# Batched matmul with bias and residual: a regrouped head, and x in two buffers of eight tiles

## The chip, the cores and the metric

The kernel runs on one core of a Trainium2 chip. The metric is the device time of one execution in microseconds; "time before" is the median of seven executions. TensorE (PE) does the products and the transposes, VectorE (DVE), ScalarE (ACT) and GpSimd (POOL) the elementwise work, and SyncE (SP) issues nearly all the DMA transfers.

## The reference

```python
batch, m, k, n = 16, 512, 1024, 768
# x [batch, m, k], weight [k, n], bias [n], residual [batch, m, n], all float32
np.matmul(x, weight) + bias + residual
```

## The kernel before, in words

The batch and row dimensions are flattened to M = 8192 rows. A tile is 128 rows, so there are 64 tiles; eight of them form a group S (eight groups). Row p*8 + j of a group goes to partition p, so one partition holds eight neighbouring rows of x (8 x 4 KB, contiguous in memory), and likewise of the residual (8 x 3 KB) and the output.

Per tile t the work is:

- `cast(t)`, line 90: ScalarE copies 128 x 1024 of x from float32 to bfloat16 into `xb` (a ring of four).
- `transp(t)`, lines 98 and 100: TensorE makes eight 128 x 128 transposes into `pt` in PSUM (a ring of two), and VectorE copies them to `xt` (a ring of four).
- `mms(t, i)` for the eight steps i, line 104: each step is a pair of products, 512 and 256 columns wide, that accumulate in `po` (a ring of three).
- `finish(t)`, lines 129 and 131, on VectorE. For t < 12 it writes product plus bias to `tmp`, and `pool_add(t)`, line 121, on GpSimd adds that to the residual in `ro`. For later tiles GpSimd has already added the bias to the residual, and VectorE adds the product to it.
- The finished group in `ro` is stored from there (line 82).

The weights are loaded in float32 into the buffer `w_st`, which borrows the fourth `ro` buffer, and cast to bfloat16 (`w_sb`) by `cast_w`, lines 181 and 183, on ScalarE or VectorE. The unit of W is a block c of 256 rows with two halves e.

Before, x sits in four buffers of half a group (`X_BUFS = 4`, `H = 4`, 16 KB a partition each) and each buffer is loaded by one 2 MiB transfer (line 68), except for the first ones, which are cut finer. The residual sits in four buffers of a group (line 76, 3 MiB each).

The order of work on each engine is the order of the program, written out by hand (`keep_in_program_order`). SP issues its transfers in that order too, each of them when what it needs is free: a load of x waits for the casts that read the buffer before, a load of the residual for the store of the group that used the buffer, and each also for the transfer that was issued eight transfers earlier.

The head treats tiles 0 to 2 together, since W arrives slowly: warm-up matmuls (`keep_warm`, line 175), the product that spreads the bias over the partitions (line 188, copied by VectorE at line 192), the first casts and transposes, and then step after step of W for three tiles. The head's order of transfers is: x of tile 0, W block 0 half 0, tiles 1 and 2, W block 0 half 1, W blocks 1 to 3, tiles 3, 4, 5, tiles 6 and 7 together, and then residual and x in turns up to tile 15 and residual group 1: 17 MiB in all. From tile 3 on the main loop runs: in the turn of tile t it casts t + 2, does the products of t with the transposes of t + 1 in the middle, and finishes t - 1.

Of the kernel before, what the change touches and what calls it, by code (L numbers as in the profile page):

```python
# [8 lines left out]
FP32 = mybir.dt.float32  # L9
BF16 = mybir.dt.bfloat16  # L10
P = 128
J = 8
H = 4
HEAD = 3
X_BUFS = 4
RO_BUFS = 4
TMP_BUFS = 4
EARLY = 12
# [4 lines left out]
def kernel(  # L23
# [8 lines left out]
    nc = tc.nc  # L32
# [3 lines left out]
    M, K = x2d.shape  # L36
    N = weight.shape[1]
    n_c = K // (2 * P)
    n_t = M // P
    n_s = n_t // J  # L40
# [3 lines left out]
    x_d = x2d.rearrange("(S p j) k -> S p j k", p=P, j=J)  # L44
    res_d = res2d.rearrange("(S p j) n -> S p j n", p=P, j=J)
    out_d = out2d.rearrange("(S p j) n -> S p j n", p=P, j=J)
    w_d = weight.rearrange("(c p e) n -> p c e n", p=P, e=2)

    const = ctx.enter_context(tc.tile_pool(name="const", bufs=1))
    sb = ctx.enter_context(tc.tile_pool(name="sb", bufs=1))  # L50
    ps = ctx.enter_context(tc.tile_pool(name="ps", bufs=1, space=bass.MemoryType.PSUM))

    def ring(pool, name, i, n, shape, dt):
        return pool.tile(shape, dt, name=name, tag=f"{name}{i % n}", bufs=1)

    def psum_o(i):
        return ring(ps, "po", i, HEAD, [P, N], FP32)

    x_sb, ro, xb, xt, po, tmp = {}, {}, {}, {}, {}, {}
    K_ = tc.keep_in_program_order  # L60


    def load_x(h, j0=0, j1=H):
        if h < n_t // H:
            if j0 == 0:
                x_sb[h] = ring(sb, "x_tile", h, X_BUFS, [P, H, K], FP32)
            S, b = divmod(h * H, J)
            K_(nc.sync.dma_start(
                out=x_sb[h][:, j0:j1, :], in_=x_d[S, :, b + j0:b + j1, :]
            ))  # L70

    def load_res(S, j0=0, j1=J):
        if S < n_s:
            if j0 == 0:
                ro[S] = ring(sb, "ro", S, RO_BUFS, [P, J, N], FP32)
            K_(nc.sync.dma_start(out=ro[S][:, j0:j1, :], in_=res_d[S, :, j0:j1, :]))

    def load_w(c, e0=0, e1=2):
        K_(nc.sync.dma_start(out=w_st[:, c, e0:e1, :], in_=w_d[:, c, e0:e1, :]))

    def store(S, j0=0, j1=J, n0=0, nl=N):
        K_(nc.sync.dma_start(
            out=out_d[S, :, j0:j1, n0:n0 + nl], in_=ro[S][:, j0:j1, n0:n0 + nl]
        ))


    def cast(t):
        if t < n_t:
            xb[t] = ring(sb, "xb", t, 4, [P, n_c, P, 2], BF16)
            K_(nc.scalar.copy(  # L90
                out=xb[t].rearrange("p c i e -> p (c i e)"), in_=x_sb[t // H][:, t % H, :]
            ))

    def transp(t):
        if t < n_t:
            pt = ring(ps, "pt", t, 2, [P, len(steps), P], BF16)
            for i, (c, e) in enumerate(steps):
                K_(nc.tensor.transpose(out=pt[:, i, :], in_=xb[t][:, c, :, e], identity=ident))  # L98
            xt[t] = ring(sb, "xt", t, 4, [P, len(steps), P], BF16)
            K_(nc.vector.tensor_copy(out=xt[t], in_=pt))  # L100

    def mm(t, i, n0, nl):
        c, e = steps[i]
        K_(nc.tensor.matmul(  # L104
            po[t][:, n0:n0 + nl], lhsT=xt[t][:, i, :], rhs=w_sb[:, c, e, n0:n0 + nl],
            start=(i == 0), stop=(i == len(steps) - 1),
        ))

    def mms(t, i):
        if i == 0:  # L110
            po[t] = psum_o(t)
        for n0, nl in chunks:
            mm(t, i, n0, nl)
# [4 lines left out]
    def pool_add(t):  # L118
        if 0 <= t < n_t:
            r = row(t)  # L120
            K_(nc.gpsimd.tensor_add(out=r, in0=r, in1=tmp[t] if t < EARLY else bias_sb))  # L121

    def finish(t, n0=0, nl=N):
        if t < 0:
            return
        p = po[t][:, n0:n0 + nl]
        if t < EARLY:
            tmp[t] = ring(sb, "tmp", t, TMP_BUFS, [P, N], FP32)
            K_(nc.vector.tensor_add(out=tmp[t], in0=p, in1=bias_sb))  # L129
        else:  # L130
            K_(nc.vector.tensor_add(out=row(t, n0, nl), in0=p, in1=row(t, n0, nl)))  # L131
# [4 lines left out]
    w_st = ring(sb, "ro", RO_BUFS - 1, RO_BUFS, [P, n_c, 2, N], FP32)  # L136
    w_sb = const.tile([P, n_c, 2, N], BF16, name="w_sb")

    load_x(0, 0, 1)
    load_w(0, 0, 1)  # L140
    load_x(0, 1, 2)
    load_x(0, 2, 3)
    load_w(0, 1, 2)
    load_w(1)
    load_w(2)
    load_w(3, 0, 1)
    load_w(3, 1, 2)
    load_x(0, 3, 4)
    load_x(1, 0, 1)
    load_x(1, 1, 2)  # L150
    load_x(1, 2, 4)
    load_res(0, 0, H)
    load_x(2)
    load_res(0, H, J)
    load_x(3, 0, 2)
    load_res(1, 0, H)
    load_x(3, 2, 4)
    load_res(1, H, J)

    warm = const.tile([P, 512], BF16, name="warm")  # L160
    K_(nc.vector.memset(warm, 0.0))  # L161
# [5 lines left out]
    ident = const.tile([P, P], BF16, name="ident")  # L167
    make_identity(nc, ident)
    bias_sb = const.tile([P, N], FP32, name="bias_sb")
    bias_ps = psum_o(1)  # L170
    warm_ps = psum_o(2)

    def keep_warm(n):
        for _ in range(n):
            K_(nc.tensor.matmul(  # L175
                warm_ps[:, 0:512], lhsT=warm[:, 0:P], rhs=warm, start=True, stop=True
            ))

    def cast_w(c, e, engine):
        if engine == "act":  # L180
            K_(nc.scalar.copy(out=w_sb[:, c, e, :], in_=w_st[:, c, e, :]))  # L181
        else:
            K_(nc.vector.tensor_copy(out=w_sb[:, c, e, :], in_=w_st[:, c, e, :]))  # L183


    keep_warm(6)
    for n0, nl in chunks:
        K_(nc.tensor.matmul(  # L188
            bias_ps[:, n0:n0 + nl], lhsT=ones_row, rhs=bias_row[:, n0:n0 + nl],
            start=True, stop=True,  # L190
        ))
    K_(nc.vector.tensor_copy(out=bias_sb, in_=bias_ps))  # L192
    keep_warm(4)
    cast(0)
    cast_w(0, 0, "dve")
    transp(0)
    keep_warm(3)
    cast(1)
    mms(0, 0)
    keep_warm(3)  # L200
    transp(1)
    cast(2)
    keep_warm(3)
    mms(1, 0)
    cast_w(0, 1, "dve")
    transp(2)
    mms(0, 1)
    mms(1, 1)
    mms(2, 0)
    mms(2, 1)  # L210
    cast_w(1, 1, "act")
    cast_w(1, 0, "dve")
    cast_w(2, 1, "act")
    cast_w(2, 0, "dve")
    cast_w(3, 0, "dve")
    cast_w(3, 1, "dve")
    cast(HEAD)
    load_x(X_BUFS)
    load_res(2)
    cast(HEAD + 1)  # L220
    for i in range(2, len(steps)):
        for t in range(HEAD):
# [8 lines left out]
    for t in range(HEAD, n_t):  # L231
        cast(t + 2)
        S, j = divmod(t, J)
        if (t + 2) % H == H - 1:
            load_x((t + 2) // H + X_BUFS)
            if j < H:
                load_res(S + 2)
            elif 1 <= S < n_s - 1:
                store(S - 1)
        if t < n_t - 1:  # L240
            for i in range(len(steps)):
                mms(t, i)
                if i == T_STEP:
                    transp(t + 1)
        finish(t - 1)
        if t - 1 < EARLY:
            pool_add(t - 1)
        if t + 1 >= EARLY:
            pool_add(t + 1)
        if S == n_s - 1 and j == 0:  # L250
            store(S - 1)
        if S == n_s - 1 and j == H:
            store(S, 0, H)
    t, S = n_t - 1, n_s - 1
    store(S, H, J - 1)
    po[t] = psum_o(t)
    for n0, nl in chunks:
        for i in range(len(steps)):
# [33 lines left out]
```

## Time and profile before

| | us |
|---|---|
| median of 7 executions | 214.69 |
| lowest, highest | 213.26, 219.32 |
| the profiled execution | 213.25 |
| its span in the profile | 211.5 |
| TensorE busy in the span | 201.7 (95%) |
| VectorE, ScalarE, GpSimd busy | 104.2, 69.1, 114.5 |
| bytes moved by DMA, mean rate | 87.27 MB, 413 GB/s |

The span is what the profiler sees from the first to the last event; the execution's own time is 1.75 us longer. A row of the timeline has start and busy time in us, engine, line, operation, what it writes and reads, how often, and in brackets how long the engine had stood idle and what released it. A line of the DMA queues has packets, MB, and the share of the time of 16 transfer engines.

### The profile page before, as it was taken

To read this page: it belongs to the slowest core of one execution; us is meant where nothing else is said; L and a number is where in the kernel's file an instruction comes from. 1 tells how busy PE (TensorE), PEld (TensorE's weight loads), DVE (VectorE), ACT (ScalarE), POOL (GpSimd) and SP (SyncE) were. 2 spreads that over 40 slices of the span, in tenths; PEclk is the share of its full clock that TensorE was granted. 3 is DMA by queue.
4 is the path that set the end of the run, shared out by engine and by line. 5 is a ranking of instruction groups with operands and counts; after the bars stand their busy time and mean duration, and the time that the engine had idled before them with its cause. 6 is when DMAs were issued, how large, how long until landed. Compare 5 with 4: busy or idle time off the path is not lost.

```text
span 211.5 us, 3621 instructions
## 1 busy us (share of the span) xinstructions
PE 201.7 (95%) x1529; PEld 131.3 (62%) x1559; DVE 104.2 (49%) x139; ACT 69.1 (33%) x68; POOL 114.5 (54%) x70
## 2 busy tenths in 40 slices
PE   7998999999999999999999999999999999999980
PEld 2455666666666666666666666666666666666650
DVE  0554544554455455545544554455445545544550
ACT  4435315331607233323332333233233233330000
POOL 1000097959989959910997029930599107990000
PEclk9999999999999999999999999999999999999997
DMA  6999999999999999999999999999999999999984
GB/s 216 412 414 425 436 422 422 418 435 443 418 418 445 418 429 434 412 442 417 425 420 437 435 425 429 409 451 421 408 421 428 446 415 429 406 437 425 424 341 196
DMA packets 7075, 87.27 MB, mean 413 GB/s; under 512 B 786, under 2 KB 914, under 8 KB 2579
## 3 DMA queue, kind: packets, MB, share of 16 engines
q1 hardware_dynamic: 7056, 87.03, 97.7%
q8 instruction: 12, 0.20, 0.4%
q14 instruction: 5, 0.03, 0.0%
q10 hardware_dynamic: 2, 0.00, 0.0%
HBM read 61.87 MB, written 25.17 MB: 412 GB/s over the span
## 4 chain that ended last, share of the span: by engine, by line
PE 94%; DVE 3%; issue 1%; DVEq 0%
PE po L104 78%; PE pt L98 13%; PE po L175 2%; DVE xt L100 1%; PE po L188 1%; DVE ro L131 1%; DVE bias_sb L192 0%; DVE tmp L129 0%; DVE w_sb L183 0%; DVE warm L161 0%; DVEq L131 0%
## 5 line engine op out<-in xcount | busy, mean ns | idle before, releaser
L104 PE MATMUL po<-w_sb,xt 128*128 128x256 bf16 (+1 forms) x994 | 175.1, 324 | 3.5 <-DVE ro L131 0.8
L104 PEld LDWEIGHTS <-xt 128*128 128x128 bf16 x1024 | 97.3, 98 | 61.5 <-DVE xt L100 2.0
L121 POOL TENSOR_TENSOR ro<-ro,bias_sb 128x768 f32<-128x768 f32 x52 | 92.5, 1815 | 46.3 <-DMA ro<-in_residual_dram 22.4
L90 ACT CAST xb<-x_tile 128x1024 bf16<-128x1024 f32 x64 | 65.9, 1045 | 117.2 <-PE pt L98 98.5
L100 DVE COPY xt<-pt 128x1024 bf16<-128x1024 bf16 x64 | 44.3, 692 | 94.1 <-PE pt L98 94.1
L131 DVE TENSOR_TENSOR ro<-po,ro 128x768 f32<-128x768 f32 (+2 forms) x53 | 49.4, 933 | 1.8 <-PE po L104 1.8
L98 PEld LDWEIGHTS <-xb 128*128 128x128 bf16 x512 | 34.0, 98 | 8.5
L98 PE MATMUL pt<-ident,xb 128*128 128x128 bf16 x512 | 39.0, 219 | 0.0
L121 POOL TENSOR_TENSOR ro<-ro,tmp 128x768 f32<-128x768 f32 x12 | 21.5, 1816 | 28.6 <-DMA ro<-in_residual_dram 26.2
L129 DVE TENSOR_TENSOR tmp<-po,bias_sb 128x768 f32<-128x768 f32 x12 | 11.3, 948 | 0.0
L175 PE MATMUL po<-warm 128*128 128x512 bf16 x19 | 6.2, 459 | 1.2 <-DVE warm L161 1.2
L183 DVE CAST w_sb<-ro 128x768 bf16<-128x768 f32 x6 | 3.3, 555 | 1.4 <-DMA ro<-in_weight_dram 1.4
L175 PEld LDWEIGHTS <-warm 128*128 128x128 bf16 x19 | 1.8, 110 | 3.3 <-issue 1.4
L192 DVE COPY bias_sb<-po 128x768 f32<-128x768 f32 x1 | 1.0, 957 | 4.5 <-PE po L188 4.5
L181 ACT CAST w_sb<-ro 128x768 bf16<-128x768 f32 x2 | 1.7, 832 | 2.9 <-DMA ro<-in_weight_dram 2.9
L188 PE MATMUL po<-tmp,ones_row 1*128 1x512 f32 (+1 forms) x4 | 1.8, 581 | 0.0
L188 PEld LDWEIGHTS po<-tmp,ones_row 1*128 1x128 f32 x4 | 0.9, 246 | 1.4 <-issue 1.4
L166 ACT ACT_TABLE_LOAD x1 | 1.3, 1283 | 1.3 <-PEq L276 1.3
L161 DVE MEMSET warm<- 128x256 uint32 x1 | 0.3, 272 | 0.9 <-PEq L276 0.9
masks.py:197 POOL MEMSET ident<- 128x128 bf16 x1 | 0.2, 205 | 0.3 <-POOLq L276 0.3
masks.py:199 POOL TENSOR_SCALAR_AFFINE_SELECT ident<-ident 128x128 bf16<-128x128 bf16 x1 | 0.3, 293 | 0.1
L276 POOL MEMSET const-float32-0.0<- 128x1 f32 x1 | 0.1, 98 | 0.2 <-issue 0.2
(6 smaller groups left out, 0.7 us busy)
## 6 DMA issues: line engine op xcount, KB each, us to landing
x_tile<-in_x_dram SPq DMA_DIRECT2D x13, 2048.0 KB, 23.2
out_dram<-ro SPq DMA_DIRECT2D x7, 3072.0 KB, 24.2
ro<-in_residual_dram SPq DMA_DIRECT2D x6, 3072.0 KB, 12.5
ro<-in_residual_dram SPq DMA_DIRECT2D x4, 1536.0 KB, 24.8
x_tile<-in_x_dram SPq DMA_DIRECT2D x6, 512.0 KB, 8.3
x_tile<-in_x_dram SPq DMA_DIRECT2D x3, 1024.0 KB, 22.0
ro<-in_weight_dram SPq DMA_DIRECT2D x4, 384.0 KB, 6.6
ro<-in_weight_dram SPq DMA_DIRECT2D x2, 768.0 KB, 8.5
```

What stands on the lines that cost most here:

```text
L90: K_(nc.scalar.copy(out=xb[t].rearrange("p c i e -> p (c i e)"), in_=x_sb[t // H][:, t % H, :]))
L98: K_(nc.tensor.transpose(out=pt[:, i, :], in_=xb[t][:, c, :, e], identity=ident))
L100: K_(nc.vector.tensor_copy(out=xt[t], in_=pt))
L104: K_(nc.tensor.matmul(po[t][:, n0:n0 + nl], lhsT=xt[t][:, i, :], rhs=w_sb[:, c, e, n0:n0 + nl], start=(i == 0), stop=(i == len(steps) - 1),))
L121: K_(nc.gpsimd.tensor_add(out=r, in0=r, in1=tmp[t] if t < EARLY else bias_sb))
L129: K_(nc.vector.tensor_add(out=tmp[t], in0=p, in1=bias_sb))
L131: K_(nc.vector.tensor_add(out=row(t, n0, nl), in0=p, in1=row(t, n0, nl)))
L166: K_(nc.scalar.copy(out=warm_a, in_=warm_a))
L175: K_(nc.tensor.matmul(warm_ps[:, 0:512], lhsT=warm[:, 0:P], rhs=warm, start=True, stop=True))
L181: K_(nc.scalar.copy(out=w_sb[:, c, e, :], in_=w_st[:, c, e, :]))
L183: K_(nc.vector.tensor_copy(out=w_sb[:, c, e, :], in_=w_st[:, c, e, :]))
L188: K_(nc.tensor.matmul(bias_ps[:, n0:n0 + nl], lhsT=ones_row, rhs=bias_row[:, n0:n0 + nl], start=True, stop=True,))
```

## The change

The head is regrouped:

- x of tiles 0 and 1 comes in one 1 MiB transfer with 8 KB in each partition. Tile 0 is cast by VectorE and tile 1 by ScalarE.
- Each block of W comes in one transfer with 6 KB in each partition. From each block VectorE and ScalarE cast one half; before, VectorE cast both halves of the first and the last block.
- 16 warm-up matmuls stand in front, in place of 19 spread over the head, and the bias product comes behind the transposes of tiles 0 and 1.
- Tile 2 is cast and transposed after the first two steps of tiles 0 and 1.

x then sits in two buffers of a whole group (32 KB a partition, the same memory in sum), each loaded by one 4 MiB transfer from group 2 on. The loads of x group S + 2 and residual group S + 2 are both issued in the turn of tile 8S + 5; before, the two halves of x were issued in the turns of tiles 8S + 1 and 8S + 5, the residual with the first of them, and the first such loads already in the head.

```diff
-H = 4
-X_BUFS = 4
+X_BUFS = 2
...
+    def load_x(S, j0=0, j1=J):
+        if S < n_s:
             if j0 == 0:
+                x_sb[S] = ring(sb, "x_tile", S, X_BUFS, [P, J, K], FP32)
+            K_(nc.sync.dma_start(out=x_sb[S][:, j0:j1, :], in_=x_d[S, :, j0:j1, :]))
...
+    def cast(t, engine="act"):
         if t < n_t:
             xb[t] = ring(sb, "xb", t, 4, [P, n_c, P, 2], BF16)
+            copy = nc.scalar.copy if engine == "act" else nc.vector.tensor_copy
...
-    load_x(0, 0, 1)
-    load_w(0, 0, 1)
-    load_x(0, 1, 2)
+    load_x(0, 0, 2)
+    load_w(0)
     load_x(0, 2, 3)
-    load_w(0, 1, 2)
     load_w(1)
     load_w(2)
-    load_w(3, 0, 1)
-    load_w(3, 1, 2)
+    load_w(3)
     load_x(0, 3, 4)
-    load_x(1, 0, 1)
-    load_x(1, 1, 2)
-    load_x(1, 2, 4)
-    load_res(0, 0, H)
-    load_x(2)
-    load_res(0, H, J)
-    load_x(3, 0, 2)
-    load_res(1, 0, H)
-    load_x(3, 2, 4)
-    load_res(1, H, J)
+    load_x(0, 4, 6)
+    load_x(0, 6, 8)
+    load_res(0, 0, 4)
+    load_x(1, 0, 4)
+    load_res(0, 4, 8)
+    load_x(1, 4, 6)
+    load_res(1, 0, 4)
+    load_x(1, 6, 8)
+    load_res(1, 4, 8)
...
-    bias_ps = psum_o(1)
-    warm_ps = psum_o(2)
+    warm_ps = psum_o(1)
+    bias_ps = psum_o(2)
...
-    keep_warm(6)
+    keep_warm(16)
+    cast(0, "dve")
+    cast(1)
+    transp(0)
+    transp(1)
+    cast_w(0, 0, "act")
+    cast_w(0, 1, "dve")
     for n0, nl in chunks:
         K_(nc.tensor.matmul(
             bias_ps[:, n0:n0 + nl], lhsT=ones_row, rhs=bias_row[:, n0:n0 + nl],
             start=True, stop=True,
         ))
     K_(nc.vector.tensor_copy(out=bias_sb, in_=bias_ps))
-    keep_warm(4)
-    cast(0)
-    cast_w(0, 0, "dve")
-    transp(0)
-    keep_warm(3)
-    cast(1)
     mms(0, 0)
-    keep_warm(3)
-    transp(1)
+    mms(0, 1)
+    mms(1, 0)
+    mms(1, 1)
     cast(2)
-    keep_warm(3)
-    mms(1, 0)
-    cast_w(0, 1, "dve")
     transp(2)
-    mms(0, 1)
-    mms(1, 1)
+    for c in range(1, n_c):
+        cast_w(c, 0, "dve")
+        cast_w(c, 1, "act")
     mms(2, 0)
     mms(2, 1)
-    cast_w(1, 1, "act")
-    cast_w(1, 0, "dve")
-    cast_w(2, 1, "act")
-    cast_w(2, 0, "dve")
-    cast_w(3, 0, "dve")
-    cast_w(3, 1, "dve")
     cast(HEAD)
-    load_x(X_BUFS)
-    load_res(2)
     cast(HEAD + 1)
...
-        if (t + 2) % H == H - 1:
-            load_x((t + 2) // H + X_BUFS)
-            if j < H:
-                load_res(S + 2)
-            elif 1 <= S < n_s - 1:
+        if (t + 2) % J == J - 1:
+            load_x(S + X_BUFS)
+            load_res(S + X_BUFS)
+            if 1 <= S < n_s - 1:
                 store(S - 1)
```

More of the change, by code (lines that the diff above doesn't have):

```diff
@@ L60 @@
     K_ = tc.keep_in_program_order
-    def load_x(h, j0=0, j1=H):
-        if h < n_t // H:
+    def load_x(S, j0=0, j1=J):
+        if S < n_s:
             if j0 == 0:
[L66 to L70, printed above, removed]
+                x_sb[S] = ring(sb, "x_tile", S, X_BUFS, [P, J, K], FP32)
+            K_(nc.sync.dma_start(out=x_sb[S][:, j0:j1, :], in_=x_d[S, :, j0:j1, :]))
     def load_res(S, j0=0, j1=J):
@@ L76, in load_res, with load_w @@
             K_(nc.sync.dma_start(out=ro[S][:, j0:j1, :], in_=res_d[S, :, j0:j1, :]))
-    def load_w(c, e0=0, e1=2):
-        K_(nc.sync.dma_start(out=w_st[:, c, e0:e1, :], in_=w_d[:, c, e0:e1, :]))
+    def load_w(c):
+        K_(nc.sync.dma_start(out=w_st[:, c, :, :], in_=w_d[:, c, :, :]))
     def store(S, j0=0, j1=J, n0=0, nl=N):
@@ L84, in store @@
         ))
-    def cast(t):
+    def cast(t, engine="act"):
         if t < n_t:
             xb[t] = ring(sb, "xb", t, 4, [P, n_c, P, 2], BF16)
-            K_(nc.scalar.copy(
-                out=xb[t].rearrange("p c i e -> p (c i e)"), in_=x_sb[t // H][:, t % H, :]
+            copy = nc.scalar.copy if engine == "act" else nc.vector.tensor_copy
+            K_(copy(
+                out=xb[t].rearrange("p c i e -> p (c i e)"), in_=x_sb[t // J][:, t % J, :]
             ))
@@ L251 @@
             store(S - 1)
-        if S == n_s - 1 and j == H:
-            store(S, 0, H)
+        if S == n_s - 1 and j == J // 2:
+            store(S, 0, J // 2)
     t, S = n_t - 1, n_s - 1
-    store(S, H, J - 1)
+    store(S, J // 2, J - 1)
     po[t] = psum_o(t)
```

## The prediction

> **What bounds the kernel now.** I read the busy table and the DMA queues first, because they show whether one engine or two are full; then the chain, for which of them ends last.
>
> ```profile
> PE 201.7 (95%) x1529; PEld 131.3 (62%) x1559; DVE 104.2 (49%) x139; ACT 69.1 (33%) x68; POOL 114.5 (54%) x70
> q1 hardware_dynamic: 7056, 87.03, 97.7%
> PE 94%; DVE 3%; issue 1%; DVEq 0%
> ```
>
> Both TensorE and the DMA engines are full, and the chain that ends last is TensorE's. So a change pays only if TensorE starts its unbroken work earlier, or if it is never made to wait; and any transfer that moves back in the queue may turn into a wait. Next came the timeline, which has the start of the dense stretch and the landings:
>
> ```profile
> 12.02 5.31 PEld L104 LDWEIGHTS <-xt 128*128 128x128 bf16 x34 [0.52 <-DVE xt L100]
> 16.20 1.04 ACT L90 CAST xb<-x_tile 128x1024 bf16<-128x1024 f32 x1 [2.42 <-DMA x_tile<-in_x_dram]
> 17.55 0.61 PE L98 MATMUL pt<-ident,xb 128*128 128x128 bf16 x8
> 19.81 1.46 PE L104 MATMUL po<-w_sb,xt 128*128 128x512 bf16 x7 [0.67 <-DVE tmp L129]
> 43.60 1.99 ACT L90 CAST xb<-x_tile 128x1024 bf16<-128x1024 f32 x2 [4.57 <-DMA x_tile<-in_x_dram]
> 52.19 2.94 ACT L90 CAST xb<-x_tile 128x1024 bf16<-128x1024 f32 x3 [6.60 <-PE pt L98]
> 57.67 0.61 PE L98 MATMUL pt<-ident,xb 128*128 128x128 bf16 x8
> 59.48 14.22 POOL L121 TENSOR_TENSOR ro<-ro,bias_sb 128x768 f32<-128x768 f32 x8 [1.05 <-DMA ro<-in_residual_dram]
> ```
>
> TensorE is dense from 12.02. Tile 3 lands at 16.20, is cast by 17.24 and transposed at 17.55; from tile 4 (21.11) every tile takes 3.048 us, so the transposes of tile t start at 21.11 + 3.048(t-4): 57.67 for tile 16, the row shown. The casts of tiles 14, 16 and the residual of group 2 give landings of 43.60, 52.19 and 59.48.
>
> **A ruler for landings.** Counted in queue order, these three transfers end at 15.5, 19 and 22 MiB. From 15.5 to 22 MiB it takes 15.88 us, 2.443 us a MiB; 19 MiB should then land at 52.15, and 52.19 is seen. So landings can be read off a byte count to about 0.1 us. (The row at 52.19 names PE as its releaser, but the buffer that this cast needs had been free since tile 12's transposes at 46.1; the byte count says that it was the load.)
>
> [...]
>
> **The change, part by part.** Landings in the head, interpolated between rows of the trace (tile 0, 0.5 MiB, 4.56; tile 1, 1.375 MiB, 6.91; tile 2, 1.875 MiB, 8.21; W block 1, 3.0 MiB, 11.06): the pair of tiles 0 and 1 (1.0 MiB) 5.90, W block 0 (1.75) 7.89, tile 2 (2.25) 9.16. W blocks 1 to 3 and tile 3 keep their byte counts, and so 11.06, 12.95, 14.92 and 16.20.
>
> *Two casts at once.* VectorE's cast of 1024 elements is not in the trace. [...] It ends at 6.6, ScalarE's (1.045) at 6.95. Transposes (0.61 a tile) end at 7.2 and 7.7, their copies (0.69) at 7.9 and 8.6. ScalarE casts W half 0 (0.83) by 8.7, VectorE half 1 (0.56) by 9.2.
>
> *Bias product moved.* It took 1.85 us on the clock's rise. Bounds: 0.93 if it was all at half clock, 1.85 if none; I take 1.65, so 7.7 to 9.35, ahead of the first product in TensorE's order. Its copy on VectorE (0.96) ends at 10.3 and delays nothing: tile 2's copy, behind it, is not due before 11.2. Then four pairs (0.32 each) to 10.6, tile 2's transposes (cast 9.16 to 10.2) to 11.2, the copy to 11.95: the dense stretch starts at **12.0**, as before. With the low price it is 11.6.
>
> *Warm-up matmuls*: 19 become 16, all in front. At 0.457 us cold and 0.26 warm they end near 6.4, before the first transposes; cost nothing, hidden by the first load. The nine fillers between steps go.
>
> *What follows from 12.0* is the old sequence: 10 pairs (0.64 for tile 2, then steps 2 to 6 for three tiles, 4.80) end at 17.4; tile 3 is cast by 17.25 as before. So the head gives 0 to 0.3 us, and I take 0.1. W's last half moves from VectorE to ScalarE (0.83 for 0.56): from 14.92 to 15.75, before tile 3 lands at 16.20, so it is covered. Tiles 4 and 5 as one load land at 18.8 instead of 17.5 for tile 4: cast by 19.9, due at 21.11, covered.
>
> *SP.* 43 issues become 36, 0.33 to 0.45 us each; SP mostly waits, so nothing. The loads of x group 2 and residual group 2 move from the head to the turn of tile 5. There SP waits for the cast of tile 7 (24.2), and for the transfers eight issues back (22 to 26). By 26 the queue has moved 8.5 of its first 17 MiB, so the transfer engines never run dry. Later turns: x group 4 waits for the cast of tile 23 (68.9) while the first store still occupies the queue until some 86; spare 17 us.
>
> *x in 4 MiB transfers.* This is what costs. The old order after 17 MiB was x of tiles 16 to 19 (to 19 MiB), residual 2 (22), x of 20 to 23 (24). The new one is x of 16 to 23 (21), residual 2 (24). Tile 16 lands with tile 23, 2 MiB later: 52.15 + 2 x 2.443 = 57.04. Its cast ends at 58.1 and the transposes start near 58.2, due at 57.67 (57.57 with the head's gain). **TensorE waits, and is 0.5 us later than before**; the head's gain is swallowed. Behind the waiting cast on ScalarE stand only casts of the same load.
>
> *What is late next.* Residual 2 lands at 59.48 + 4.89 = 64.4; GpSimd's add (1.8) ends at 66.2 and VectorE's at 67.15. Queued behind that on VectorE is the copy of tile 19 (due 67.9), and the products of tile 19 need both by 69.0: 1.9 us to spare. Tile 24 lands at 28 MiB, 74.2, due 82.05. The late groups, counted from the old landing of tile 56 (168.68, 66 MiB), arrive near 149 for tile 48 (due 155.2) and 173.6 for tile 56 (due 179.6). No more waits; the tail's stores are unchanged.
>
> Sum against the profiled execution of 213.25 us (span 211.5 and 1.75 around it): head -0.1, tile 16 +0.6, the rest 0: +0.5, 213.7. The median shown is 1.44 above that execution; some of its excess may be slower transfers, where both kernels wait for the same bytes, so I carry 0.4: **215.1**.
>
> **Rivals.** An effect within 0.5% (1.07 us) could not be told from no change.
> - *The gain is kept.* If x group 2 lands by 56.4 instead of 57.04, tile 16 doesn't wait and the head's 0.3 remains: 214.4. For it: the 8 KB and 6 KB rows of the head, where the trace has only 377 to 397 GB/s from 3 to 7 us. Against it: the rows of 4 KB and 3 KB around 14 to 17 us ran at 410 to 422, so row size is not the reason.
> - *Transfers get faster altogether.* [...]TensorE caps it at the median's excess plus the head, 1.44 + 0.27: 213.0. Against it: the loads of 16 KB rows and the residuals of 24 KB rows moved at the same 427 to 430.
> - *The 4 MiB load lands later than its count* (slower). Landing lagged the bytes by 0.9 us at the start and by 2.6 at 52 us[...]. At the cast of tile 16 every us of it is a us of TensorE. From 0.6 us beyond my estimate it decides for slower; with another 1.7 of lag tile 16 waits 2.2, 216.9. For it: no slack there. Against it: the ruler held to 0.1 us.
> - *The clock falls* without the nine fillers. [...] Against it: from 6.6 to 12 TensorE's longest pause is 0.7 us.
> - *The two casts do not run early.* The shared load lands 1.3 us after tile 0 alone did, so "at once" buys tile 1 and costs tile 0; that is in the sum already.
>
> **Chances.** Main case 0.50 (215.1, same), gain kept 0.10 (same), faster transfers 0.12 (faster), late landing 0.20 (slower), clock 0.08 (slower): faster 0.12, same 0.60, slower 0.28. The range goes from 213.6, half way into the case of faster transfers, to 216.9, the late landing.
>
> **What would show it.** Right: dense work from about 12, tile 3's transposes at 17.3 to 17.6, a wait of ScalarE for x that ends near 57, TensorE's transposes of tile 16 near 58.2 and then 3.048 a tile to the end. Wrong: a second wait of the transposes for x after 60 us, VectorE idle for GpSimd near 66, a granted clock or matmul length at half speed between 6 and 12[...].

## The result, and the profile after

The changed kernel takes 211.83 us (median of 12 executions, 211.64 to 212.41). The kernel before, measured beside it and earlier, takes 215.35 (31 executions, 213.07 to 219.32). The ratio is 0.986, with a 95% interval of 0.9834 to 0.9886: faster by 1.4%. (Ratios here leave out executions over 1.5% above the fastest of their kernel, so they can differ from the quotient of the medians, 0.984.) The forecast was 215.1, within a range of 213.6 to 216.9, with 0.12 on faster by over 0.5%.

The busy table, the main DMA queue and the chain of the changed kernel look like those of before, apart from fewer packets; nothing in these totals tells where the time went:

```profile
PE 201.3 (96%) x1526; PEld 131.2 (62%) x1556; DVE 103.9 (49%) x138; ACT 69.1 (33%) x69; POOL 114.5 (55%) x70
q1 hardware_dynamic: 5616, 87.03, 97.5%
PE 96%; DVE 1%; issue 1%; DVEq 0%
```

The times of the kernel before lie at several levels: 4 of its 31 executions at 213.1 to 213.3 us, ten at 214.6 to 214.9, thirteen at 215.2 to 215.9 and four from 216.65 to 219.32. The execution shown ahead of the prediction (213.25) was one of the quick four. A second profile of the same kernel caught the commonest level, where the median lies too (215.45 us; called the usual one here); the level at 214.6 was not profiled. The two profiles part at the head of TensorE's timeline. The columns are start, busy time, engine, line, operation, shapes, count. First the usual execution of the kernel before:

```profile
1.19 2.74 PE L175 MATMUL po<-warm 128*128 128x512 bf16 x6 [1.19 <-DVE warm L161]
3.85 2.92 PE L188 MATMUL po<-tmp,ones_row 1*128 1x512 f32 x4
6.71 1.89 PE L175 MATMUL po<-warm 128*128 128x512 bf16 x4
8.39 1.06 PE L98 MATMUL pt<-ident,xb 128*128 128x128 bf16 x8
9.25 1.48 PE L175 MATMUL po<-warm 128*128 128x512 bf16 x3
12.10 0.61 PE L98 MATMUL pt<-ident,xb 128*128 128x128 bf16 x8
14.27 6.64 PE L104 MATMUL po<-w_sb,xt 128*128 128x512 bf16 x37
20.75 0.61 PE L98 MATMUL pt<-ident,xb 128*128 128x128 bf16 x8
```

Then the same rows of the quick execution of that kernel:

```profile
3.86 1.85 PE L188 MATMUL po<-tmp,ones_row 1*128 1x512 f32 x4
5.64 1.04 PE L175 MATMUL po<-warm 128*128 128x512 bf16 x4
6.51 0.61 PE L98 MATMUL pt<-ident,xb 128*128 128x128 bf16 x8
```

And the changed kernel (its line 168 is the warm-up, 187 the bias product, 95 the transposes, 101 the products):

```profile
1.19 5.82 PE L168 MATMUL po<-warm 128*128 128x512 bf16 x16 [1.19 <-DVE warm L154]
6.84 1.05 PE L95 MATMUL pt<-ident,xb 128*128 128x128 bf16 x16
7.83 1.55 PE L187 MATMUL po<-tmp,ones_row 1*128 1x512 f32 x4
12.02 5.70 PE L101 MATMUL po<-w_sb,xt 128*128 128x512 bf16 x33 [0.79 <-DVE xt L97]
17.56 0.61 PE L95 MATMUL pt<-ident,xb 128*128 128x128 bf16 x8
```

The length of eight transposes is the clock's gauge: 1.06 us at half clock (after_warm6, below, has this length at 11.77, where the granted clock is 0.50) and 0.61 at full (at 17.56 in the changed kernel, granted 1.00). In the usual execution of the kernel before, the bias product takes 2.92 us instead of 1.85 and the transposes of tile 0 still take 1.06 at 8.39; only those at 12.10 run at full clock. Tile 3 is transposed at 20.75, against 17.55 in the quick execution and 17.56 in the changed kernel. That 3.2 us of TensorE stays to the end, as the last rows of the chain show (VectorE's last addition; usual before, quick before, after):

```profile
209.62 0.42 DVE ro L131
```

```profile
206.42 0.42 DVE ro L131
```

```profile
206.44 0.42 DVE ro L128
```

The usual execution is longer than the quick one by 2.2 us only, since the quick one has to wait for its transfers at the end (383 GB/s from 206 to 208 us, where the usual one moves 18). The changed kernel and the quick execution of the old one end TensorE's work at the same moment, and yet the first is 1.4 us shorter. The table by stretch shows why; its last two columns are the share and the rate (GB/s) of the transfers. Quick before:

```profile
200.00:204.00 4.00, 3.95 (x29) 2.41 (x28) 2.43 (x4) 0.00 (x0) 0.00 (x0) 1.00 0.87 364
204.00:206.00 2.00, 1.15 (x10) 0.68 (x8) 0.69 (x1) 0.00 (x0) 0.00 (x0) 1.00 0.80 336
```

After:

```profile
200.00:204.00 4.00, 3.95 (x29) 2.39 (x29) 2.46 (x4) 0.00 (x0) 0.00 (x0) 1.00 0.59 252
204.00:206.00 2.00, 1.15 (x9) 0.69 (x8) 0.69 (x1) 0.00 (x0) 0.00 (x0) 1.00 0.70 295
```

In the old kernel the queue still has a backlog of stores to move when the last ones are issued; in the new one it has nearly run out, and they land sooner. So there are two limits: TensorE's start, which makes the 2.2 us between the two profiles of the kernel before, and the queue's end, which makes the 1.4 us between the quick one and the changed kernel. The rows that answer to the forecast's other steps, in the changed kernel, are these:

```profile
56.57 5.91 ACT L87 CAST xb<-x_tile 128x1024 bf16<-128x1024 f32 x6 [11.53 <-PE po L101]
57.67 0.62 PE L95 MATMUL pt<-ident,xb 128*128 128x128 bf16 x8
63.74 14.22 POOL L118 TENSOR_TENSOR ro<-ro,bias_sb 128x768 f32<-128x768 f32 x8 [5.32 <-DMA ro<-in_residual_dram]
```

### The profile page after: what moved, and what is told of

It is laid out like the page before. It is cut to its first block, busy times and chain, and to the rows that moved or that the text cites. A ratio compares the mean times of both kernels' runs of the same rounds, so it can differ in the third digit from the quotient of the medians.

```text
span 210.1 us, 3594 instructions
## 1 busy us (share of the span) xinstructions
PE 201.3 (96%) x1526; PEld 131.2 (62%) x1556; DVE 103.9 (49%) x138; ACT 69.1 (33%) x69; POOL 114.5 (55%) x70
## 4 chain that ended last, share of the span: by engine, by line
PE 96%; DVE 1%; issue 1%; DVEq 0%
PE po L101 79%; PE pt L95 14%; PE po L168 3%; PE po L187 1%; DVE ro L128 1%; DVE tmp L126 0%; DVE xt L97 0%; DVE warm L154 0%; DVEq L128 0%
## 5 line engine op out<-in xcount | busy, mean ns | idle before, releaser
L87 ACT CAST xb<-x_tile 128x1024 bf16<-128x1024 f32 x63 | 64.3, 1045 | 116.3 <-PE pt L95 70.0
L174 ACT CAST w_sb<-ro 128x768 bf16<-128x768 f32 x4 | 3.3, 832 | 3.8 <-DMA ro<-in_weight_dram 3.8
L176 DVE CAST w_sb<-ro 128x768 bf16<-128x768 f32 x4 | 2.2, 554 | 1.3 <-DMA ro<-in_weight_dram 1.3
L87 DVE CAST xb<-x_tile 128x1024 bf16<-128x1024 f32 x1 | 0.7, 694 | 4.2 <-DMA x_tile<-in_x_dram 4.2
```

The lines of the kernel that those rows point to most:

```text
L87: K_(copy(out=xb[t].rearrange("p c i e -> p (c i e)"), in_=x_sb[t // J][:, t % J, :]))
```

## The experiments

Each was measured beside the kernel before, whose median was 214.85, 215.42 and 214.81 us in the three sets; the changed kernel was not measured again, so its 211.83 us comes from another set than the runs put beside it. From the first pair of profiles, whose TensorE ends alike, the gain looked like one of transfers, and the first four runs were built on that: the **rows** theory (32 KB rows of x move faster), the **order** theory (x, residual and store of a group together), and as a rival the **head** (TensorE starts earlier). The **clock** theory (the old head leaves TensorE at half clock longer in most executions) came with the first of these runs.

**The kernel before, again** (no edit; label before_again).

> The kernel before, unchanged, for a second profile: the first fell on one of its quick executions (213.25 against a median of 215.35). Transfer theory (the queue of transfers, not TensorE, sets the end of a usual execution): TensorE's last product ends within 0.3 us of the first profile's 206.4, the transfers from 200 to 206 us stay above 400 GB/s, and the last store lands 1.5 to 3 us later than in the first profile. TensorE theory (a usual execution has waits of TensorE that the first profile lacks): TensorE's last product ends 1.5 us or more later.

215.45 us. TensorE ends 3.2 us later than in the first profile, and the transfers have run dry by then: 184 GB/s from 204 to 206 us and 18 from 206 to 208. For this execution the transfer theory falls and TensorE's holds.

**The new head with the old body** (head_only).

```diff
-X_BUFS = 2
+X_BUFS = 4
+H = 4
...
-        if (t + 2) % J == J - 1:
-            load_x(S + X_BUFS)
-            load_res(S + X_BUFS)
+        if (t + 2) % H == H - 1:
+            load_x((t + 2) // H + X_BUFS)
+            if j < H:
+                load_res(S + 2)
...
```

> The changed kernel's head, with the old body: x in four buffers of 16 KB a partition, loaded in 2 MiB transfers, residual and x of group 2 issued in the head as before. Row-length theory (the transfers of x in rows of 32 KB take less time than those of 16 KB, 768 rows of 1219 ns for 1536 of 625 ns, some 1.5 us on 16 engines; the head's longer rows give 0.5 us): most of the gain is missing, 214.3 us (213.3 to 215.4). Head theory (the gain is the head's earlier start): 211.8, as the changed kernel.

212.69 us (212.17 to 213.31; ratio 0.9907, 0.9874 to 0.994). Most of the gain is the head's (2.2 us below the median of its set, against 3.5 for the whole change), and the upper levels are gone. The row-length theory expected 214.3 and fails here.

**The old head with the new body** (body_only).

```diff
-X_BUFS = 4
+X_BUFS = 2
...
-    load_x(X_BUFS)
-    load_res(2)
...
+        if (t + 2) % J == J - 1:
+            load_x(S + X_BUFS)
+            load_res(S + X_BUFS)
...
```

> The old head (transfers, casts, warm-up and bias as before), with the new body: x in two buffers of 32 KB a partition, from group 2 on in 4 MiB transfers, issued where the changed kernel issues them. Row-length theory: 1.5 of 2.0 us of transfer time saved, 212.4 us (211.8 to 213.3). Head theory: 215.0, as before. Order theory (it is the order of loads and stores that helps, not the rows): also 212, so this run does not tell row length from order; the run with 16 KB rows does.

214.48 us (ratio 0.9963, 0.9925 to 1.0001), with the levels again: 4 of 14 executions at 212.2 to 212.9, the others from 214.4. The body alone gains little, since in the usual execution TensorE, late by its clock, covers the transfers (123 GB/s from 204 to 206 us in this profile, of 215.24 us). At the quick level it gains up to 0.9 us against the first four quick executions of before (213.1 to 213.3); the one of its own set, 212.42, leaves next to nothing, so the size is open here.

**The same transfers in 16 KB rows** (rows_16k).

```diff
+ROW = 4
+PAD = 16
...
-                x_sb[S] = ring(sb, "x_tile", S, X_BUFS, [P, J, K], FP32)
+                x_sb[S] = ring(sb, "x_tile", S, X_BUFS, [P, J // ROW, ROW * K + PAD], FP32)
...
```

> The changed kernel with 64 bytes of padding in the middle of each x buffer, so that each partition's 32 KB arrive as two rows of 16 KB. Same transfers, same order, same waits, same bytes. Row-length theory: 1.5 us of transfer time comes back, of which the changed kernel's tail can hide about 1: 212.6 us (212.0 to 214.5), with 16 KB packets near 625 ns. Order theory and the theory that fewer, larger transfers help: 211.8, no change.

211.86 us, no change, although its packets are 6402 against 5634. The time alone is a weak witness, since in the changed kernel transfers have slack (leaving out a whole store changes nothing there, below). The packets of the traces say more. 80 MiB have landed at 199.2 us here, at 198.8 in the changed kernel and at 200.1 in head_only, and the stretch in which these part, from 60 to 78 MiB, takes 43.8, 43.9 and 45.3 us. The length of x's rows is not the main reason; 0.4 us of transfer time for it can't be excluded.

**Six warm-up matmuls in the changed kernel** (after_warm6).

```diff
-    keep_warm(16)
+    keep_warm(6)
```

> The changed kernel with 6 warm-up matmuls in front in place of 16; nothing else differs. Clock theory[...]: TensorE stands still from 3.8 to 5.5 us, the clock rises later in most executions, the dense stretch starts near 14, and the time is 213.5 to 215 us, with a wider spread than the changed kernel's 0.8 us. Transfer and body theory: 211.8, no change, since no transfer moves.

216.22 us (214.22 to 217.43; ratio to the kernel before 1.0072, 1.0037 to 1.0107): 4.4 us more than with 16, slower than the kernel before. Here the clock shows in the granted column too (the third from the right, ahead of share and rate):

```profile
0.00:5.29 5.29, 2.74 (x6) 0.73 (x6) 0.41 (x3) 1.47 (x2) 0.70 (x6) 1.00 0.66 243
5.29:10.60 5.31, 4.54 (x25) 2.39 (x26) 3.41 (x5) 3.14 (x4) 0.00 (x0) 0.74 1.02 425
10.60:16.00 5.40, 4.61 (x21) 2.38 (x20) 2.10 (x4) 2.85 (x4) 0.00 (x0) 0.50 1.02 420
```

The clock had risen once, for the sixteen transposes of tiles 0 and 1 (1.07 us at 6.07), and fell back (eight in 1.06 at 11.77). No transfer was touched, so the loss is TensorE's: in this profile, of 215.60 us, its last addition starts at 210.17 for 206.44. The loss was larger than the 1.7 to 3.2 us expected.

**Only the bias product moved, in the kernel before** (bias_moved).

```diff
     keep_warm(6)
+    keep_warm(4)
+    cast(0)
+    cast_w(0, 0, "dve")
+    transp(0)
     for n0, nl in chunks:
...
     K_(nc.vector.tensor_copy(out=bias_sb, in_=bias_ps))
-    keep_warm(4)
-    cast(0)
-    cast_w(0, 0, "dve")
-    transp(0)
     keep_warm(3)
```

> The kernel before with one thing moved: the two matmuls of the bias product and their copy stand behind the transposes of tile 0 and no longer between the first six and the next four warm-up matmuls. The number of warm-up matmuls, the transfers and the body are those of before. Clock theory, with the bias product as what breaks the stretch: most executions reach the full clock before 8 us, the usual time falls from 215.4 to 212.8 us (212.2 to 213.8), and the wide spread of before is gone or smaller. Theory that it is the number of warm-up matmuls ahead of the first load: 10 in a row are still short of 16, 214 us. Transfer theory: 215, as before.

213.32 us (ratio 0.994, 0.9918 to 0.9962), and 15 of 22 executions lie between 212.65 and 213.6, where only 6 of 51 of the kernel before do in the same set. One move of two matmuls is worth 2.1 us by the medians, 1.3 by the ratio. It does so by making the quick level the common one: tile 3 is transposed at 17.80, no earlier than in the quick execution of before. In the profile the ten warm-up matmuls stand in one piece, the transposes of tile 0 take 0.62 and the bias product 1.55:

```profile
1.19 4.26 PE L175 MATMUL po<-warm 128*128 128x512 bf16 x10 [1.19 <-DVE warm L161]
5.47 0.62 PE L98 MATMUL pt<-ident,xb 128*128 128x128 bf16 x8
6.02 1.55 PE L192 MATMUL po<-tmp,ones_row 1*128 1x512 f32 x4
```

**Sixteen warm-up matmuls in the old head** (warm_first).

```diff
-    keep_warm(6)
+    keep_warm(16)
     for n0, nl in chunks:
...
     K_(nc.vector.tensor_copy(out=bias_sb, in_=bias_ps))
-    keep_warm(4)
     cast(0)
```

> The kernel before with 16 warm-up matmuls in front of the bias product in place of 6, and without the 4 behind it; transfers, casts, the other fillers and the body as before. Clock theory: full clock by about 7 us in every execution, 212.8 us (212.2 to 213.5), spread under 1.5 us. Theory that the paired load and the two casts bring the gain: 215, as before.

214.87 us, ratio 1.0003: the expectation of the clock theory was missed by 2 us. The level is the old one: 13 of 14 executions lie between 214.2 and 215.7, and none is quick. The head of its profile shows why: the clock is full (0.62 for eight transposes), but the warm-up ends at 7.4 us, the bias product still stands ahead of the transposes of tile 0, and they start at 8.82 instead of 6.51; tile 3 comes at 20.66, as in the usual execution of before. So this head gained nothing by the longer warm-up. The new head pairs it with a load that lands at 5.50 us and puts the bias product behind; in the changed kernel its transposes start at 6.84.

The execution profiled was the fourteenth, of 219.26 us, and it shows what the longest times are. TensorE ends as in the usual execution (last addition at 209.52), but the queue does not run dry:

```profile
204.00:206.00 2.00, 2.00 (x20) 1.37 (x18) 1.39 (x2) 0.00 (x0) 0.00 (x0) 1.00 0.98 418
208.00:210.00 2.00, 1.03 (x8) 0.68 (x7) 0.82 (x2) 0.00 (x0) 0.00 (x0) 1.00 0.99 421
```

From 100 to 200 us it moved 404 GB/s, where the usual execution of before moved 424. Here the transfers and not the clock make the time long. Executions of the kernel before at 219 us were not profiled.

**The new head and old body, less one store** (head_only_less).

```diff
-            elif 1 <= S < n_s - 1:
+            elif 2 <= S < n_s - 1:
                 store(S - 1)
```

> The new head with the old body, and without the store of group 0 (3 MiB less to move; that group of the output is not written). Tail theory (with the clock mended, the old body's transfers still set the end, since they are not through before the last stores): 3 MiB are 7 us of transfer time, the last stores land at once, 211.6 us or less, against 212.7 with the store. Theory that TensorE alone sets the end: 212.7, no change.

It leaves group 0 of the output unwritten. 211.89 us (211.53 to 212.57), against 212.69 with the store (in another set), and the queue is dry at the end (slices of 148 and 180 GB/s). So with the new head and the old body the transfers do set the end, by 0.8 us.

**The changed kernel, less the same store** (after_less).

```diff
-            if 1 <= S < n_s - 1:
+            if 2 <= S < n_s - 1:
                 store(S - 1)
```

> The changed kernel without the store of group 0 (3 MiB less to move; that group of the output is not written). Theory that TensorE alone sets its end: 211.8 us, no change (211.5 to 212.1). Theory that transfers still reach into its tail: 211.3 or less.

It, too, leaves group 0 of the output unwritten. 211.92 us: no change. In the changed kernel TensorE alone sets the end. In this profile the clock happened to rise early (the 16 warm-up matmuls take 4.97 us for 5.82), the dense stretch starts at 11.52, and the wait that the forecast placed at tile 16 becomes visible (3.27 us from tile to tile where 3.05 is usual):

```profile
54.13 0.61 PE L95 MATMUL pt<-ident,xb 128*128 128x128 bf16 x8
57.40 0.62 PE L95 MATMUL pt<-ident,xb 128*128 128x128 bf16 x8
```

**The moved bias product with the new body** (bias_body).

```diff
 (bias_moved, and the body of body_only)
-X_BUFS = 4
+X_BUFS = 2
```

> The old head with only the bias product moved behind the transposes of tile 0 (as in the run where that alone was moved, 213.32 us), now with the new body (x in two buffers of 32 KB, one 4 MiB transfer a group). Theory of two parts (clock 2.1 us, the rest from the body's transfers, which no longer reach into the tail): 212.2 us (211.8 to 212.7). Theory that the new head's paired load and two casts bring that rest: 213.3, no change from the body.

212.71 us (ratio 0.9927, 0.9902 to 0.9953): between the two theories' numbers, which it does not decide. 14 of 22 executions lie at 212.3 to 213.1, and eight at 213.9 to 214.2; in the profile of one of the latter the clock has risen for the transposes of tile 0 (0.62) and is back at half for the next fillers (three in 1.46 us against 0.81). In that execution ten warm-up matmuls did not keep the clock at full. The lower level is some 0.6 below that of bias_moved, measured in another set.

**Two half loads in place of each 4 MiB load** (x_halves).

```diff
-            load_x(S + X_BUFS)
+            load_x(S + X_BUFS, 0, 4)
+            load_x(S + X_BUFS, 4, 8)
```

> The changed kernel with each 4 MiB load of x issued as two 2 MiB loads of tiles 0 to 3 and 4 to 7 of the group, back to back, in the same two buffers. Each of them reads 16 KB of every 32 KB, as the old body's loads do; order of groups and waits as in the changed kernel. Theory that it is the transfer that reads every second 16 KB that is slow now and then (in the old body's profiles some 25 packets of 16 KB lie together at over 0.8 us): 212.5 us (212.2 to 213), with such packets in the profile. Theory that it is the order of the loads and stores (x, residual and store of a group together): 211.8, no change.

211.91 us, no change, and again 43.8 us for the bytes from 60 to 78 MiB. Neither x's rows nor the size of the loads explains the body's gain; what is left is its order, the moments of issue included.

A count over the traces fits: packets of 16 KB or more in the main queue that took over 1.35 times 0.0374 ns a byte (the usual pace of the large ones) number 44, 51, 46 and 47 in the kernel before (both profiles), head_only and bias_moved, and 11, 12, 15, 13 and 11 in the changed kernel, body_only, rows_16k, x_halves and bias_body. Their excess is 1.05 to 1.48 us of each engine's time in the old order and 0.33 to 0.44 in the new. In the old order they lie in clumps, 26 of them between 170 and 180 us in head_only. The execution of 219.26 us of warm_first, also in the old order, has 167 of them, with an excess of 5.6 us: that one is long by slow packets, not by the clock. Why the old order has these clumps was not found.

The head has a part in the transfers as well. The first 17 MiB have landed at 45.1 to 45.3 us in the six profiles with the old head's loads, at 44.5 to 44.7 in the eight with the new ones: half a microsecond, whatever the body. The new loads are fewer and have longer rows; which of the two does it was not separated. With the 0.9 us that the bytes from 60 to 78 MiB save (44.8 us in the quick execution of before, 43.9 in the changed kernel) it accounts for the 1.4 us between these two profiles.

**A version that beats both** (best).

```diff
     mms(0, 0)
     mms(0, 1)
+    cast(2)
+    transp(2)
     mms(1, 0)
     mms(1, 1)
-    cast(2)
-    transp(2)
...
-            load_x(S + X_BUFS)
+            if S == 0:
+                load_x(2, 0, 4)
+                load_x(2, 4, 8)
+            else:
+                load_x(S + X_BUFS)
```

> The changed kernel with two edits: the transposes of tile 2 come before the products of tile 1, so that TensorE has those products to do while VectorE copies tile 2 (it stood still there for 0.79 us), and the 4 MiB load of x group 2 is issued in two halves, so that tile 16 lands some 5 us sooner and does not stop the earlier TensorE at its transposes. If TensorE alone sets the end and both edits are needed: 0.7 us less than the changed kernel, 211.1 us (210.8 to 211.5). If the transfers in the tail are next: 211.6. If the casts of tile 3 or the first residual hold it: 211.8, no change.

211.08 us (five of six executions between 211.00 and 211.17; ratio to the kernel before 0.9855, 0.9807 to 0.9903), 0.75 below the changed kernel's 211.83 and 0.83 below x_halves of the same set. Since x_halves gains nothing, the halved load is worth nothing by itself; the moved transposes were not run alone. The pause of 0.79 us is gone, tile 16 lands at 51.5 and its transposes run at 56.68, a full 3.05 behind tile 15's:

```profile
10.08 6.65 PE L101 MATMUL po<-w_sb,xt 128*128 128x512 bf16 x37
51.50 3.89 ACT L87 CAST xb<-x_tile 128x1024 bf16<-128x1024 f32 x4 [6.60 <-DMA x_tile<-in_x_dram]
53.63 0.61 PE L95 MATMUL pt<-ident,xb 128*128 128x128 bf16 x8
56.68 0.61 PE L95 MATMUL pt<-ident,xb 128*128 128x128 bf16 x8
```

## Why the prediction was wrong

- **The step that failed first is the excess of the median, 1.44 us, "where both kernels wait for the same bytes".** With 0.4 carried on the median of 214.69 the changed kernel was given nearly all of it. It got none: its profiled execution took 211.86, its median is 211.83. In the usual execution of the kernel before the transfers run dry (184 and 18 GB/s), and TensorE is 3.2 us late (tile 3 at 20.75 for 17.55), since its clock rises late (eight transposes still take 1.06 us at 8.39); with the 16 warm-up matmuls of the new head no profile shows that (sixteen transposes behind them take 1.05 to 1.07 us in six profiles). The start of the dense stretch, "12.0, as before", was right for the changed kernel (12.02) and for one quick execution of the other: the sum set an unusual "before" against a usual "after". The clue was in the profile: "1.85 us on the clock's rise" in the bias product (2.92 in the usual execution, 1.55 in the changed kernel), and seven executions from 213.3 to 219.3 said that something changes from one to the next (the longest, by warm_first, more likely by slow packets).
- **The second is "the rest 0".** Against the quick execution itself +0.5 was forecast and -1.4 measured (211.86 for 213.25), with the last addition at the same moment. The transfers end 1.4 us sooner, a term put at nothing because rows of 16 KB and 24 KB had moved alike (427 to 430 GB/s); the order of the loads and the head's loads were not priced. The three terms together, 1.4 for the excess, 1.4 for the transfers and 0.5 for tile 16, are the 3.3 us between 215.1 and 211.83.
- **The warm-up matmuls**, which "cost nothing", were priced, 16 for 19, by their time. Their worth is in what the clock does after them: 6 and a gap cost 4.4 us in the new head.
- **The rival on the clock had the wrong sign.** It took the nine fillers for the protection and their loss for the danger. The weak point, by bias_moved, was the bias product between the first six and the next four (213.32 us with it moved, 215.42 without). What a fall of the clock would cost, the trace of before did not show. The rise varies from run to run (16 warm-up matmuls in 4.94 to 6.44 us); the forecast took the one rise it saw for the rule.
- **Tile 16.** Landing 57.04 was forecast, 56.57 seen. The ruler was right: with the old head's loads and the new order, in bias_body, it is met to 0.01 us.

```profile
57.03 3.89 ACT L87 CAST xb<-x_tile 128x1024 bf16<-128x1024 f32 x4 [10.93 <-DMA x_tile<-in_x_dram]
```

What was missed is the 0.5 us of the new head's loads. The rival "the gain is kept" had named them, and the sum dismissed it because row size had seemed not to matter between 14 and 17 us; from 4 to 8 us the new head moves 411 to 417 GB/s, the old 380 to 410. The transposes came at 57.67, in time by a hair. In after_less, with an earlier start, the wait is there (0.22 us): mechanism right, landing about 0.5 us too late. Residual 2 landed at 63.74 for 64.4, and no wait followed, as forecast.
- **The two casts.** The pair landed at 5.50, not 5.90; VectorE's cast took 0.694 (the forecast has 0.7, from 5.90 to 6.6: the author's estimate), the bias product 1.55 (1.65). Tile 2's chain ended where the forecast had it.
- **The faster case** had its number (213.0) from transfers capped by TensorE. By how much transfers could quicken, the trace of before did not show (it has 423 GB/s from 22 to 41 us and 433 from 41 to 57; the changed kernel has 425 and 438). Transfers did become quicker, by 1.4 us at the end, though in the main not through the length of x's rows. That is the smaller part; the other is the 2.2 us of the clock, which no case had with this sign.
- **Two slips** without effect: from 12.0 there are 17 pairs of products, not 10 (their 5.44 us are right), and the DMA lists have 49 issues of SP before and 39 after, not 43 and 36.

## What to carry to other kernels

Before a forecast, ask whether the profiled execution is a usual one: where the times have several levels, find which stage differs, and price the change against the usual one. In this kernel the warm-up paid as one piece of 16 full-size matmuls with the bias product behind it: in six profiles with the new head the clock had risen when they ended, after 4.94 to 6.44 us, and the changed kernel took 211.83 us, where it took 216.22 with six matmuls. In warm_first, where the bias product and the transposes of tile 0 had to wait for it, the same piece gained nothing (214.87). When two limits lie within a per cent (here TensorE's start and the queue's end), mending one shows only as much as the other allows.

## What was not expected of the hardware

- Being busy did not suffice for the full clock: in the usual execution of the kernel before TensorE is shown as busy without a break from 1.19 to 12 us, and still ran at half clock to about 11 us (eight transposes in 1.06 us at 8.39, three fillers in 1.48 at 9.25 and, at full clock, in 0.81 at 12.54). The bias product, whose operands fill one row, lies in this stretch. That it delays the rise is inferred from bias_moved (eight transposes in 0.62 us at 5.47 ahead of it); neither its single row nor its type (float32) was varied by itself.
- The granted clock of the profile stands at 1.00 in that stretch; the length of the matmuls shows the half clock (eight transposes in 1.06 us, the length they also have in after_warm6 where the column shows 0.50).
- The 16 warm-up matmuls, the same in each program, took 4.94 us in the profile of head_only, 5.82 in the changed kernel's and 6.44 in that of x_halves; in all of them the transposes that follow ran at full clock (sixteen in 1.05 to 1.07 us).
